# One PSUM chain for six of the seven products: the channel mixer's second matrix product, regrouped

## The chip, the cores and the metric

The kernel runs on one core of one Trainium2 chip. The metric is the device time in microseconds of one execution. Its engines work beside each other and meet by semaphores: PE (matrix products; PEld is its loading of weights), DVE and ACT (elementwise work, both can read PSUM), POOL (here mostly the issue of accumulating DMAs), and SP (the issue of plain DMAs). PSUM has 8 banks of 128 x 512 float32.

## The reference, cut to what matters

One layer on 512 tokens of 1024 channels: four token mixers, a gate, an output projection, then the channel mixer and the input embedding. The change is in the channel mixer's second product.

```python
hn = rms_norm(h, norm2_g[i])
ff = jnp.square(jax.nn.relu(jnp.einsum('bsd,df->bsf', hn, w_ff1[i])))
h = h + jnp.einsum('bsf,fd->bsd', ff, w_ff2[i])          # 512 x 4096 times 4096 x 1024

hg = rms_norm(h, norm3_g[i])
ple_gate = jax.nn.sigmoid(jnp.einsum('bsd,de->bse', hg, w_ple_gate[i]) + b_ple_gate[i])
h = h + ple_gate * jnp.einsum('bsq,qd->bsd', p[i], w_ple[i])
```

## The kernel before, in words

Float32 products are made of three: each operand is split into a high half that PE can multiply at full rate and a low half (the rest), and hi x hi, hi x lo and lo x hi are summed in PSUM. A weight is loaded as a tile of 128 x 1024; `split_piece` has ACT copy the high half (`wh<-raw` or `wh<-grow`, line 231) and DVE subtract it from the tile for the low half (`wl`, line 218).

The 4096 rows of `w_ff2` are worked in four groups g of 1024. In a group, the activations are a 2 x 2 grid of blocks (a11, a12, a21, a22: token half, row half), the weights too (11, 12, 21, 22: row half, column half), and the four blocks of the result take seven products of blocks, Q1 to Q7, instead of eight. A product multiplies one block or one sum of activations (`USES`; s1 to s4 are sums, made on DVE by `make`, then split into a tile `combo`) by one weight or one sum of weights (`SUMS`). A product is one step of 24 matmuls of 512 columns, on two weight tiles (h = 0, 1) and into two banks (i = 0, 1, a token block each).

The weights' sums are made by the DMAs: `load_piece` has SP load the first block plainly, and POOL add each further block with an accumulating DMA onto the same tile. `ONTO` lets a sum grow out of the tile of an earlier product once that is split: Q1 to Q5 to Q6 to Q4. Such tiles live in a ring of three (`grow`); all others in a ring of four (`raw`, `RAW = 4`), so that a plain load goes out when the low half of the fourth `raw` tile before it is made. SP and POOL each issue in the program's order.

`CHAIN` says which products share banks: a later product of a chain accumulates onto what the earlier one left. Before, Q1 and Q2 are chain 1; Q6, Q7 and Q4 chain 2; Q5 and Q3 chain 3. After each product `evac` adds the two banks onto the result tiles `ht[tb, half]` (tb: token block, half: columns) on DVE. Q1 alone is needed in six places, so its sum is kept over groups 0 to 2 (`first_q`), spread by six adds at the end of group 2 (`spread_q1`), and in group 3 spread from PSUM by six adds at once.

The order of the steps is written out: in groups 0 to 2 by `ORDER`, where the F steps are pieces of the first product of the next group; in group 3, the last, by `ORDER_LAST`, where U0 and U1 are the halves of the embedding's product `p W_p` (24 matmuls into four banks each, copied out by ACT). `MAKE` and `MAKE_LAST` say in which step an operand is made. In the middle of each step (`middle`) the low half of that operand follows, and up to two weights ahead are split.

Of the kernel before, what the change touches and what calls it, by code (L numbers as in the profile page):

```python
# [6 lines left out]
F32 = mybir.dt.float32  # L7
# [42 lines left out]
        "Q3": ("22",), "Q4": ("11", "12", "22", "21")}  # L50
ONTO = {"Q5": "Q1", "Q6": "Q5", "Q4": "Q6"}
ORDER = "Q1 F0 Q2 F1 Q5 F2 F3 Q6 F4 F5 Q7 F6 Q3 F7 Q4".split()
ORDER_LAST = "Q1 Q5 Q2 U0 Q6 Q3 Q7 U1 Q4".split()

MAKE = {"Q1": "s1", "Q2": "s2", "Q5": "s3", "F3": "s4", "Q6": "n22", "F5": "next a11", "Q4": "next a12"}
MAKE_LAST = {"Q1": "a12", "Q5": "s2", "Q2": "s4", "U0": "s3", "Q6": "n22"}
USES = {"Q1": "a11", "Q2": "a12", "Q5": "s1", "Q6": "s2", "Q7": "s3", "Q3": "s4", "Q4": "n22"}

# [20 lines left out]
def layout():  # L81


    out = []
    loads = []
    at = {}

    def flush():
        for i in range(len(at.setdefault("done", [])), len(out)):
            at["done"].append(i)  # L90
            loads.append(((i,), out[i][-1], None))

    tok = lambda n: [("tok", "w_in", COL[n], 512, (2 * i, 2 * i + 1), 1024) for i in range(4)]
    ch = lambda n, m: ("ch", "w_in", COL[n] + 128 * m, 1024)
    out += tok("a_v")
    out += [("gka", i, 816 if i < 2 else 544) for i in range(3)]
    out += tok("g_v")
    for m in range(4):
        out += [ch("a_q", m), ch("a_k", m)]
    for m in range(4):  # L100
        out += [ch("c_g", m), ch("c_a", m)]
    out += [ch("g_q", m) for m in range(2)]
    out += [ch("g_r", m) for m in range(4)]

    def branch(n):
        for m in range(8):
            out.append(("gate", n, m, 1024))
            if m % 2 == 0:
                out.append(("br", n, m // 2, 1024))

    branch(2)
    out += tok("sg_v")
    out += [ch("sg_u", m) for m in range(2)]
    flush()
    last = {}
    blocks = {}
    for p, e in gate_steps():
        if p == "S":
            out.append(ch("sg_u", e))
            flush()  # L120
        elif p[0] == "B":
            if int(p[1]) % 2 == 0:
                out.append(("br", e[0], 2 * e[1] + int(p[1]) // 2, 1024))
                flush()
        else:
            if p == "Q5":
                for b in ("11", "12", "21", "22"):
                    blocks[b] = len(out)
                    out.append(("gblock", *e, int(b[0]) - 1, int(b[1]) - 1, 1024))
                    at["done"].append(blocks[b])  # L130
            old = GATE_ONTO.get(p)
            new = GATE_SUMS[p][len(GATE_SUMS[old]) if old else 0:]
            loads.append((tuple(blocks[b] for b in new), 1024, last[old] if old else None))
            last[p] = len(loads) - 1
    out += [("ch", "w_out", 128 * m, 1024) for m in range(8)]
    flush()
    ff1 = lambda g, m: ("ch", "w_ff1", 1024 * g + 128 * m, 1024)
    out += [ff1(0, m) for m in range(8)]
    flush()
    for g in range(4):  # L140
        blocks = {}
        for e in ("11", "12", "21", "22"):
            for h in range(2):
                blocks[e, h] = len(out)
                out.append(("ff2", g, int(e[0]) - 1, int(e[1]) - 1, h, 1024))
                at["done"].append(blocks[e, h])
        last = {}
        for e in ORDER if g < 3 else ORDER_LAST:
            if e[0] == "F":
                out.append(ff1(g + 1, int(e[1])))  # L150
                flush()
            elif e[0] == "U":
                out.append(("tok", "w_ple", 512 * int(e[1]), 512, (0, 1), 1024))
                flush()
            else:
                for h in range(2):
                    old = ONTO.get(e) if g < 3 or e != "Q5" else None
                    new = SUMS[e][len(SUMS[old]) if old else 0:]
                    loads.append((tuple(blocks[n, h] for n in new), 1024, last[old, h] if old else None))
                    last[e, h] = len(loads) - 1  # L160
    for half in range(2):
        out += [("tok", "w_ple_gate", 512 * half, 512, (2 * i, 2 * i + 1), 1024) for i in (2, 3, 0, 1)]
    flush()
    return out, loads
# [9 lines left out]
def build(tc, x, w, vec, wa2, sgw, rows, rb, pt, out):  # L174
# [55 lines left out]
    def copy(o, a, **k):  # L230
        return ACT.activation(o, a, AF.Copy, **k)  # L231
# [1025 lines left out]
    def block(g, i, k):  # L1257

        return act[g, k][:, :, 256 * i:256 * i + 256]

    def make(g, n):

        sign = None
        if n == "a11":
            src = block(g, 0, 0)
        elif n == "a12":
            src = block(g, 0, 1)
        elif n == "n22":
            src, sign = block(g, 1, 1), -1.0
        else:  # L1270
            if n in ("s1", "s3"):
                combos[n] = lpool.tile([128, 4, 256], F32, tag=n, bufs=1, name=name(n))
            src = combos["s3" if n == "s3" else "s1"]
            if n == "s1":
                tt(src, block(g, 1, 0), block(g, 1, 1), OP.subtract)
            elif n == "s2":
                tt(src, block(g, 0, 0), src, OP.subtract)
            elif n == "s3":
                tt(src, block(g, 1, 0), block(g, 0, 0), OP.subtract)
            else:  # L1280
                tt(src, block(g, 0, 1), src, OP.subtract)
        t = lpool.tile([128, 2, 4, 256], F32R, tag="combo", bufs=4, name=name("combo"))
        if sign is None:
            copy(t[:, 0], src)
        else:
            copy(t[:, 0], src, scale=sign)
        yield "mid"
        if sign is None:
            tt(t[:, 1], src, t[:, 0].bitcast(F32), OP.subtract)
        else:  # L1290
            stt(t[:, 1], src, sign, t[:, 0].bitcast(F32), OP.mult, OP.subtract)
        combos[g, n] = t

    chains = {}
    CHAIN = {"Q1": 1, "Q2": 1, "Q5": 3, "Q3": 3, "Q6": 2, "Q7": 2, "Q4": 2}
    first_q = {}

    def add_to(tb, half, b, op=OP.add):
        tt(ht[tb, half], ht[tb, half], b, op)

    def spread_q1(i, t):
        add_to(i, 1, t, OP.subtract)
        add_to(2 + i, 1, t, OP.subtract)
        add_to(2 + i, 0, t)

    def product(g, n):
        j = base[n, g]
        c = CHAIN[n]
        fresh = n in ("Q1", "Q5", "Q6")

        def mms(_):
            if fresh:
                for i in range(2):
                    chains[c, i] = bank()
            t = combos.pop((g, USES[n]))
            for h in range(2):
                if h:
                    middle()
                hi, lo = parts[j + h]
                for i in range(2):  # L1320
                    b = chains[c, i]
                    for k in range(2):
                        s = [t[:, q, 2 * h + k, 128 * i:128 * i + 128] for q in range(2)]
                        cs = slice(512 * k, 512 * k + 512)
                        last = h == 1 and k == 1
                        mm(b, s[0], hi[:, cs], fresh and h == 0 and k == 0, False, skip_group_check=True)
                        mm(b, s[0], lo[:, cs], False, False, skip_group_check=True)
                        mm(b, s[1], hi[:, cs], False, last, skip_group_check=True)

        def evac(_):  # L1330
            for i in range(2):
                b = chains[c, i]
                if n == "Q1":
                    if g == 0:
                        first_q[i] = H()
                        copy(first_q[i], b)
                    elif g < 3:
                        tt(first_q[i], first_q[i], b, OP.add)
                    else:
                        spread_q1(i, b)  # L1340
                elif n == "Q2":
                    add_to(i, 0, b)
                elif n == "Q5":
                    add_to(2 + i, 1, b)
                elif n == "Q6" or n == "Q3":
                    add_to(i, 1, b)
                elif n == "Q7":
                    add_to(2 + i, 1, b)
                else:
                    add_to(2 + i, 0, b, OP.subtract)  # L1350

        step(j + 1, mms, evac, own=False)

# [58 lines left out]
    for g in range(4):  # L1412
        for e in ORDER if g < 3 else ORDER_LAST:
# [10 lines left out]
            else:  # L1424
                product(g, e)
            if g == 2 and e == "Q1":
                for i in range(2):
                    spread_q1(i, first_q.pop(i))
                start(load_last())
            if g == 2 and e == "F7":  # L1430
                hg = None
# [188 lines left out]
```

## Time and profile before

| what | value |
|---|---|
| runs: median of 3 (lowest to highest) | 986.85 us (986.17 to 987.85) |
| profiled execution | 986.83 us |
| its span in the trace | 985.1 us |
| PE busy | 965.7 us, 98% |
| DVE, ACT, POOL busy | 685.1, 457.6, 98.7 us |
| mean granted clock of PE | 0.994 of full |

The profiled execution is one run; its span is what the trace covers. A busy PE is not a PE at its peak, since records of matmuls overlap; the pace is read from where matmuls start. The group that the change touches most, the last one, begins near 876 us and ends with Q4 near 929 us.

### The profile page before, as it was taken

The page shows a single profiled execution, that of the slowest core. Times are in us where ns is not written, and L with a number is a line of the kernel's source. Part 1 is how long each engine was busy: PE and PEld are TensorE (multiplying, and loading weights), DVE is VectorE, ACT ScalarE, POOL GpSimd, SP SyncE. Part 2 cuts the span into 40 slices and gives each one's busy share as a digit, 9 for nine tenths or more (in the row PEclk, how much of TensorE's full clock was granted, in tenths as well). Part 3 has the DMA queues.
Part 4 walks back from the last instruction along what each step waited for, and adds up shares of the span by engine and source line. Part 5 has one row for each costly group of instructions (what it writes and reads, how often), then busy time and mean ns, then how long its engine had stood idle before and what let it go on. Part 6 is the DMA issues. An engine that isn't in the chain of part 4 may idle for free.

```text
span 985.1 us, 12890 instructions
## 1 busy us (share of the span) xinstructions
PE 965.7 (98%) x4990; PEld 820.5 (83%) x4990; DVE 685.1 (70%) x993; ACT 457.6 (46%) x685; POOL 98.7 (10%) x119
## 2 busy tenths in 40 slices
PE   8999999999999999999999999999999999999995
PEld 6977888887888898998999888888888888887885
DVE  7744897477899877877676653566576577578656
ACT  6563774235363435454554434435343345335633
POOL 5001000002121201110110000010001002011000
PEclk9999999999999999999999999999999999999998
DMA  6334322248598538756884233466468268677302
GB/s 242 121 117 128 118 82 81 86 111 188 110 237 229 141 107 199 182 168 157 220 250 129 89 129 104 92 145 170 129 171 193 99 179 183 199 176 185 133 22 86
DMA packets 43225, 144.96 MB, mean 147 GB/s; under 512 B 4859, under 2 KB 5276, under 8 KB 43164
## 3 DMA queue, kind: packets, MB, share of 16 engines
q1 hardware_dynamic: 32156, 104.29, 31.4%
q0 software_dynamic: 11008, 39.85, 22.3%
q8 instruction: 39, 0.64, 0.3%
q14 instruction: 22, 0.18, 0.1%
HBM read 139.92 MB, written 2.10 MB: 144 GB/s over the span
## 4 chain that ended last, share of the span: by engine, by line
PE 87%; DVE 6%; ACT 3%; issue 2%; DMA 1%; POOL 0%; SPq 0%; POOLq 0%; ACTq 0%; DVEq 0%
PE b L236 85%; DVE wl L218 2%; PE b L240 2%; DVE u L218 1%; ACT wh L231 1%; DVE ht L218 1%; DMA stack<-stack 1%; DVE u L222 0%; DMA raw<-w 0%; DVE gb L218 0%; DVE s L218 0%; ACT combo L231 0%; ACT ga L938 0%; DVE ht L222 0%; ACT u L231 0%
## 5 line engine op out<-in xcount | busy, mean ns | idle before, releaser
L236 PE MATMUL b<-x,wh 128*128 128x512 f32 (+1 forms) x1440 | 315.6, 363 | 2.5 <-DVE gb L218 2.5
L236 PEld LDWEIGHTS b<-x,wh 128*128 128x128 f32 x1440 | 243.9, 189 | 44.2 <-issue 4.5
L218 DVE TENSOR_TENSOR wl<-raw,wh 128x1024 fp32r<-128x1024 f32 (+2 forms) x150 | 182.3, 1223 | 74.3 <-ACT wh L231 73.0
L231 ACT ACTIVATE wh<-raw 128x1024 fp32r<-128x1024 f32 (+2 forms) x166 | 169.5, 1040 | 26.8 <-DMA raw<-w 18.4
L236 PE MATMUL b<-x,wl 128*128 128x512 f32 (+1 forms) x720 | 168.2, 361 | 0.0
L236 PE MATMUL b<-wh,combo 128*128 128x512 f32 x448 | 141.7, 390 | 0.5 <-DVE ht L218 0.5
L236 PEld LDWEIGHTS b<-x,wl 128*128 128x128 f32 x720 | 123.9, 189 | 20.8
L236 PEld LDWEIGHTS b<-wh,combo 128*128 128x128 f32 x448 | 84.1, 188 | 18.3 <-issue 0.9
L1240 ACT ACTIVATE act<-act 128x512 f32<-128x512 f32 x32 | 20.2, 632 | 147.7 <-DVE act L222 147.7
L236 PE MATMUL b<-wl,combo 128*128 128x512 f32 x224 | 87.5, 391 | 0.9 <-DVE wl L218 0.9
L236 PE MATMUL b<-u,wh 128*128 128x512 f32 x320 | 83.6, 391 | 0.0
L222 DVE SCALAR_TENSOR_TENSOR u<-pad,vecs,u 128x512 f32<-128x512 f32 x120 | 83.0, 745 | 0.0
L294 POOL DMA_DIRECT2D grow<-w x42 | 38.0, 953 | 361.6 <-DVE wl L218 307.3
L218 DVE TENSOR_TENSOR wl<-grow,wh 128x1024 fp32r<-128x1024 f32 x48 | 57.9, 1221 | 22.1 <-ACT wh L231 22.1
L236 PEld LDWEIGHTS b<-u,wh 128*128 128x128 f32 x320 | 59.3, 188 | 12.2 <-issue 0.3
L236 PE MATMUL b<-wh,x 128*128 128x512 f32 (+1 forms) x208 | 61.1, 374 | 0.0
L222 DVE SCALAR_TENSOR_TENSOR act<-b,v 128x512 f32<-128x512 f32 x32 | 22.0, 690 | 53.6 <-PE b L236 53.4
L236 PE MATMUL b<-wh,u 128*128 128x512 f32 (+1 forms) x192 | 54.1, 365 | 1.3 <-ACT wh L231 1.3
L231 ACT ACTIVATE wh<-grow 128x1024 fp32r<-128x1024 f32 x48 | 48.8, 1047 | 9.1 <-PE b L236 6.1
L236 PEld LDWEIGHTS b<-wl,combo 128*128 128x128 f32 x224 | 42.1, 188 | 10.7 <-DVE wl L218 2.1
L236 PE MATMUL b<-u,wl 128*128 128x512 f32 x160 | 46.7, 389 | 0.0
L236 PEld LDWEIGHTS b<-wh,x 128*128 128x128 f32 x208 | 38.1, 188 | 6.8
(196 smaller groups left out, 1177.4 us busy)
## 6 DMA issues: line engine op xcount, KB each, us to landing
raw<-w SPq DMA_DIRECT2D x161, 512.0 KB, 4.4
grow<-w POOLq DMA_DIRECT2D x42, 512.0 KB, 7.9
wl<-w POOLq DMA_DIRECT2D x16, 512.0 KB, 8.0
grow<-w SPq DMA_DIRECT2D x14, 512.0 KB, 5.6
raw<-w POOLq DMA_DIRECT2D x14, 512.0 KB, 7.5
h<-x SPq DMA_DIRECT2D x16, 256.0 KB, 6.9
v<-rb SPq DMA_DIRECT2D x8, 256.0 KB, 4.0
stack<-stack POOLq DMA_DIRECT2D x8, 256.0 KB, 3.7
```

The source lines that it names most:

```text
L218: return DVE.tensor_tensor(o, a, b, op=op)
L222: return DVE.scalar_tensor_tensor(o, a, s, b, op0=op0, op1=op1)
L231: return ACT.activation(o, a, AF.Copy, **k)
L236: PE.matmul(o, l, r, start=start, stop=stop, **k)
L240: PE.transpose(o, i, ident)
L294: POOL.dma_start(t[:, 0:n], w[i, :, 0:n], accum_op=OP.add)
L1240: ACT.activation(a, a, AF.Square)
```

## The change

Q1 now opens chain 2, in front of Q6, Q7 and Q4, and Q2 stands alone in chain 1. What Q1 is needed for is then in the chain's banks when Q6, Q7 and Q4 are evacuated, and every product is evacuated by two adds; `spread_q1` and `first_q` go. Q6 and Q7 are subtracted and Q4 is added; s2, s3 and s4 change sign or form to suit, and a22 is used in place of its negative. The last group's order is Q1 Q2 U0 Q5 Q6 Q3 Q7 U1 Q4 instead of Q1 Q5 Q2 U0 Q6 Q3 Q7 U1 Q4, its sums are made in other steps, and in it only Q4's weight sums still grow, out of Q6's: Q5's and Q6's are loaded on their own.

```diff
-ORDER_LAST = "Q1 Q5 Q2 U0 Q6 Q3 Q7 U1 Q4".split()
+ORDER_LAST = "Q1 Q2 U0 Q5 Q6 Q3 Q7 U1 Q4".split()
...
-MAKE_LAST = {"Q1": "a12", "Q5": "s2", "Q2": "s4", "U0": "s3", "Q6": "n22"}
-USES = {"Q1": "a11", "Q2": "a12", "Q5": "s1", "Q6": "s2", "Q7": "s3", "Q3": "s4", "Q4": "n22"}
+MAKE_LAST = {"Q1": "a12", "Q2": "s2", "U0": "s4", "Q5": "s3", "Q6": "a22"}
+USES = {"Q1": "a11", "Q2": "a12", "Q5": "s1", "Q6": "s2", "Q7": "s3", "Q3": "s4", "Q4": "a22"}
...
-                    old = ONTO.get(e) if g < 3 or e != "Q5" else None
+                    old = ONTO.get(e) if g < 3 or e == "Q4" else None
...
-                tt(src, block(g, 0, 0), src, OP.subtract)
+                tt(src, src, block(g, 0, 0), OP.subtract)
             elif n == "s3":
-                tt(src, block(g, 1, 0), block(g, 0, 0), OP.subtract)
+                tt(src, block(g, 0, 0), block(g, 1, 0), OP.subtract)
             else:
-                tt(src, block(g, 0, 1), src, OP.subtract)
+                tt(src, src, block(g, 0, 1), OP.add)
...
-        if sign is None:
-            tt(t[:, 1], src, t[:, 0].bitcast(F32), OP.subtract)
-        else:
-            stt(t[:, 1], src, sign, t[:, 0].bitcast(F32), OP.mult, OP.subtract)
+        tt(t[:, 1], src, t[:, 0].bitcast(F32), OP.subtract)
...
-    CHAIN = {"Q1": 1, "Q2": 1, "Q5": 3, "Q3": 3, "Q6": 2, "Q7": 2, "Q4": 2}
-    first_q = {}
+    CHAIN = {"Q2": 1, "Q1": 2, "Q6": 2, "Q7": 2, "Q4": 2, "Q5": 3, "Q3": 3}
...
-    def spread_q1(i, t):
-        add_to(i, 1, t, OP.subtract)
-        add_to(2 + i, 1, t, OP.subtract)
-        add_to(2 + i, 0, t)
...
-        fresh = n in ("Q1", "Q5", "Q6")
+        fresh = n in ("Q1", "Q2", "Q5")
...
-                if n == "Q1":
-                    if g == 0:
-                        first_q[i] = H()
-                        copy(first_q[i], b)
-                    elif g < 3:
-                        tt(first_q[i], first_q[i], b, OP.add)
-                    else:
-                        spread_q1(i, b)
-                elif n == "Q2":
+                if n in ("Q1", "Q2"):
                     add_to(i, 0, b)
                 elif n == "Q5":
                     add_to(2 + i, 1, b)
-                elif n == "Q6" or n == "Q3":
+                elif n == "Q6":
+                    add_to(i, 1, b, OP.subtract)
+                elif n == "Q3":
                     add_to(i, 1, b)
                 elif n == "Q7":
-                    add_to(2 + i, 1, b)
+                    add_to(2 + i, 1, b, OP.subtract)
                 else:
-                    add_to(2 + i, 0, b, OP.subtract)
+                    add_to(2 + i, 0, b)
...
             if g == 2 and e == "Q1":
-                for i in range(2):
-                    spread_q1(i, first_q.pop(i))
                 start(load_last())
```

POOL's accumulating DMAs of the last group. Before: first Q5's two weights, then the same two tiles grown for Q6, Q7's two, and the tiles grown again for Q4. The numbers tell tiles apart; what stands behind "waits" are semaphores, DMAHW of a plain load, DMASW of an accumulate, DVE of a low half.

```order
L294 DMA grow1286_7451<-w 128x1024 [waits DMAHW5_49]
L294 DMA grow1289_7458<-w 128x1024 [waits DMAHW6_49,DMASW6_49,DVE_49]
L294 DMA grow1286_7451<-w 128x1024 [waits DMASW0_49,DVE_49]
L294 DMA grow1289_7458<-w 128x1024 [waits DMASW1_49,DVE_49]
L294 DMA raw1321_7660<-w 128x1024 [waits DMAHW0_49,DMAHW2_49,DMASW5_49,DMAHW4_49,DMASW4_49,DVE_49]
L294 DMA raw1324_7667<-w 128x1024 [waits DMAHW5_49,DMAHW3_49,DMAHW7_49,DMAHW1_49,DVE_49]
L294 DMA grow1286_7451<-w 128x1024 [waits DMASW2_49,DVE_49]
L294 DMA grow1289_7458<-w 128x1024 [waits DMASW7_49,DMASW3_49,DVE_49]
```

The same stretch on POOL in the changed kernel: Q5's two (raw1296, raw1299), Q6's four (grow1305, grow1308), Q7's two, and Q4's two.

```order
L294 DMA raw1296_7519<-w 128x1024 [waits DMAHW4_49,DMAHW0_49,DVE_49]
L294 DMA raw1299_7526<-w 128x1024 [waits DMAHW1_49,DMAHW5_49,DMASW4_49,DVE_49]
L294 DMA grow1305_7564<-w 128x1024 [waits DMAHW2_49]
L294 DMA grow1305_7564<-w 128x1024 [waits DMASW2_49]
L294 DMA grow1308_7572<-w 128x1024 [waits DMAHW3_49,DMASW6_49]
L294 DMA grow1308_7572<-w 128x1024 [waits DMASW5_49,DMASW4_49]
L294 DMA raw1326_7661<-w 128x1024 [waits DMAHW6_49,DMASW0_49,DVE_49]
L294 DMA raw1333_7701<-w 128x1024 [waits DMASW7_49,DMAHW7_49,DMASW1_49,DVE_49]
L294 DMA grow1305_7564<-w 128x1024 [waits DMASW3_49,DVE_49]
L294 DMA grow1308_7572<-w 128x1024 [waits DMASW5_49,DVE_49]
```

Eight became ten; Q6's second accumulate on a tile stands directly behind the first on that tile and waits for a DMASW semaphore, not for DVE. On SP the plain loads stand in the order of the pieces: Q2's, U0's, Q5's two into `raw`, Q6's two into `grow`, Q3's two into `raw`; before it was Q5's two into `grow`, Q2's, U0's, Q3's.

DVE's work from Q1's step of the last group to the next product's evacuation. Before: the low half of operand a12, the low halves of two weights, the six adds of Q1's evacuation, then s2 and its low half, two weights, and the two adds of Q5's evacuation.

```order
L218 TENSOR_TENSOR combo1302_7551<-act1270_7327,combo1302_7551 128x1024
L218 TENSOR_TENSOR wl1306_7569<-grow1289_7458,wh1305_7568 128x1024
L218 TENSOR_TENSOR wl1308_7574<-raw1293_7492,wh1307_7573 128x1024
L218 TENSOR_TENSOR ht1018_5744<-ht1018_5744,b1303_7553 128x512
L218 TENSOR_TENSOR ht1029_5823<-ht1029_5823,b1303_7553 128x512
L218 TENSOR_TENSOR ht1004_5660<-ht1004_5660,b1303_7553 128x512
L218 TENSOR_TENSOR ht1024_5784<-ht1024_5784,b1304_7554 128x512
L218 TENSOR_TENSOR ht1043_5879<-ht1043_5879,b1304_7554 128x512
L218 TENSOR_TENSOR ht1012_5704<-ht1012_5704,b1304_7554 128x512
L218 TENSOR_TENSOR s11294_7508<-act1220_7044,s11294_7508 128x1024
L218 TENSOR_TENSOR combo1309_7597<-s11294_7508,combo1309_7597 128x1024
```

The same place on DVE in the changed kernel, to the two adds of Q2's evacuation.

```order
L218 TENSOR_TENSOR combo1300_7543<-act1268_7319,combo1300_7543 128x1024
L218 TENSOR_TENSOR wl1304_7561<-raw1287_7449,wh1303_7560 128x1024
L218 TENSOR_TENSOR wl1307_7569<-raw1291_7482,wh1306_7568 128x1024
L218 TENSOR_TENSOR ht991_5575<-ht991_5575,b1301_7545 128x512
L218 TENSOR_TENSOR ht998_5620<-ht998_5620,b1302_7546 128x512
L218 TENSOR_TENSOR s11292_7498<-s11292_7498,act1218_7036 128x1024
L218 TENSOR_TENSOR combo1309_7591<-s11292_7498,combo1309_7591 128x1024
L218 TENSOR_TENSOR wl1313_7609<-raw1296_7519,wh1312_7608 128x1024
L218 TENSOR_TENSOR wl1316_7615<-raw1299_7526,wh1315_7614 128x1024
L218 TENSOR_TENSOR ht991_5575<-ht991_5575,b1310_7593 128x512
L218 TENSOR_TENSOR ht998_5620<-ht998_5620,b1311_7594 128x512
```

Four adds are gone in front of s2, and the low halves of Q5's two accumulated weights (raw1296, raw1299) now stand in front of Q2's two adds.

## Rows read from the trace of the kernel before

**Rows 1.** The page's first part: busy time, share of the span, instructions.

```profile
PE 965.7 (98%) x4990; PEld 820.5 (83%) x4990; DVE 685.1 (70%) x993; ACT 457.6 (46%) x685; POOL 98.7 (10%) x119
```

**Rows 2.** A window: us; busy us of PE, PEld, DVE, ACT, POOL; clock, DMA, GB/s.

```profile
760.00:820.00 60.00, 60.00 (x267) 49.67 (x266) 39.62 (x45) 22.68 (x26) 3.54 (x4) 1.00 0.50 143
```

**Rows 3.** Waits of PE, 640 to 940 us: us in total, times, longest.

```profile
PE b L236 <- DVE wl L218: 0.9, 1, 0.9
PE b L236 <- DVE ht L218: 0.5, 1, 0.5
```

**Rows 4.** Timeline, 875 to 917 us: start, us, engine, what [idle before <- releaser].

```profile
875.61 1.22 DVE L218 TENSOR_TENSOR wl<-raw,wh 128x1024 fp32r<-128x1024 f32 x1
...
877.09 0.61 PE L236 MATMUL b<-wh,combo 128*128 128x512 f32 x2
...
877.77 0.61 PE L236 MATMUL b<-wh,combo 128*128 128x512 f32 x2
...
882.48 3.67 DVE L218 TENSOR_TENSOR ht<-ht,b 128x512 f32<-128x512 f32 x6
...
890.82 0.19 PEld L236 LDWEIGHTS b<-wl,combo 128*128 128x128 f32 x1 [1.25 <-DVE wl L218]
...
893.45 0.39 PE L236 MATMUL b<-wh,h 128*128 128x512 f32 x1
...
898.77 1.28 DVE L218 TENSOR_TENSOR ht<-ht,b 128x512 f32<-128x512 f32 x2
...
899.60 0.47 PE L236 MATMUL b<-wh,combo 128*128 128x512 f32 x1 [0.55 <-DVE ht L218]
...
916.67 0.39 PE L236 MATMUL b<-wh,h 128*128 128x512 f32 x1
```

**Rows 5.** Groups of instructions, 640 to 985 us: busy us, mean ns | idle before.

```profile
L218 DVE TENSOR_TENSOR wl<-raw,wh 128x1024 fp32r<-128x1024 f32 x56 | 67.2, 1219 | 15.7 <-ACT wh L231 15.6
L231 ACT ACTIVATE wh<-raw 128x1024 fp32r<-128x1024 f32 x56 | 56.6, 1048 | 5.0 <-PE b L236 3.7 <-DMA raw<-w 1.2
...
L218 DVE TENSOR_TENSOR ht<-ht,b 128x512 f32<-128x512 f32 x54 | 34.9, 680 | 0.9
...
L218 DVE TENSOR_TENSOR s<-act,s 128x1024 f32<-128x1024 f32 x8 | 9.7, 1215 | 0.0
```

**Rows 6.** The page's third part: DMA queue, packets, MB, share of 16 engines.

```profile
q1 hardware_dynamic: 32156, 104.29, 31.4%
q0 software_dynamic: 11008, 39.85, 22.3%
```

**Rows 7.** Plain loads (line 289) issued in the window 781.8 to 783.7 us.

```profile
L289 SPq DMA_DIRECT2D raw<-w x4: 382/403/729, 782.2 to 783.6; - x4
...
L289 SPq DMA_DIRECT2D grow<-w x1: 327/327/327, 781.8 to 781.8; - x1
...
DMA to landing us min/median/max: 3.6/5.2/7.8
```

**Rows 8.** SP's timeline from 870 us: the plain loads issued next.

```profile
876.85 15.41 SPq L289 DMA_DIRECT2D raw<-w  x4
```

**Rows 9.** The accumulate (line 294) issued at 857.6 us, alone.

```profile
DMA to landing us min/median/max: 5.4/5.4/5.4
```

**Rows 10.** The four accumulates (line 294) issued in the window 893 to 900 us.

```profile
DMA to landing us min/median/max: 5.7/7.3/9.6
```

**Rows 11.** POOL's timeline: the first and the last of those four.

```profile
894.87 0.88 POOL L294 DMA_DIRECT2D raw<-w  x1 [12.28 <-DVE s L218]
...
899.15 0.88 POOL L294 DMA_DIRECT2D grow<-w  x1 [0.26 <-DVE wl L218]
```

**Rows 12.** Windows near the start and at the end; columns as in rows 2.

```profile
8.00:11.20 3.20, 3.20 (x9) 2.46 (x9) 1.90 (x2) 2.72 (x5) 1.32 (x1) 0.50 1.04 408
11.20:20.00 8.80, 8.80 (x40) 7.28 (x39) 8.80 (x7) 8.80 (x14) 8.38 (x5) 1.00 0.71 260
...
977.00:980.00 3.00, 0.00 (x0) 0.00 (x0) 1.81 (x6) 0.93 (x3) 0.00 (x0) 0.52 0.23 87
```

More of the change, by code (lines that the diff above doesn't have):

```diff
@@ L52 @@
 ORDER = "Q1 F0 Q2 F1 Q5 F2 F3 Q6 F4 F5 Q7 F6 Q3 F7 Q4".split()
-ORDER_LAST = "Q1 Q5 Q2 U0 Q6 Q3 Q7 U1 Q4".split()
-MAKE = {"Q1": "s1", "Q2": "s2", "Q5": "s3", "F3": "s4", "Q6": "n22", "F5": "next a11", "Q4": "next a12"}
-MAKE_LAST = {"Q1": "a12", "Q5": "s2", "Q2": "s4", "U0": "s3", "Q6": "n22"}
-USES = {"Q1": "a11", "Q2": "a12", "Q5": "s1", "Q6": "s2", "Q7": "s3", "Q3": "s4", "Q4": "n22"}
+ORDER_LAST = "Q1 Q2 U0 Q5 Q6 Q3 Q7 U1 Q4".split()
+MAKE = {"Q1": "s1", "Q2": "s2", "Q5": "s3", "F3": "s4", "Q6": "a22", "F5": "next a11", "Q4": "next a12"}
+MAKE_LAST = {"Q1": "a12", "Q2": "s2", "U0": "s4", "Q5": "s3", "Q6": "a22"}
+USES = {"Q1": "a11", "Q2": "a12", "Q5": "s1", "Q6": "s2", "Q7": "s3", "Q3": "s4", "Q4": "a22"}
 GATES = ((1, 0), (1, 1), (0, 0), (0, 1), (3, 0), (3, 1))
@@ L1261, in make @@
     def make(g, n):
[L1263 to L1269, printed above, removed]
+        if n[0] == "a":
+            src = block(g, int(n[1]) - 1, int(n[2]) - 1)
         else:
@@ L1276, in make @@
             elif n == "s2":
-                tt(src, block(g, 0, 0), src, OP.subtract)
+                tt(src, src, block(g, 0, 0), OP.subtract)
             elif n == "s3":
-                tt(src, block(g, 1, 0), block(g, 0, 0), OP.subtract)
+                tt(src, block(g, 0, 0), block(g, 1, 0), OP.subtract)
             else:
-                tt(src, block(g, 0, 1), src, OP.subtract)
+                tt(src, src, block(g, 0, 1), OP.add)
         t = lpool.tile([128, 2, 4, 256], F32R, tag="combo", bufs=4, name=name("combo"))
-        if sign is None:
-            copy(t[:, 0], src)
-        else:
-            copy(t[:, 0], src, scale=sign)
+        copy(t[:, 0], src)
         yield "mid"
-        if sign is None:
-            tt(t[:, 1], src, t[:, 0].bitcast(F32), OP.subtract)
-        else:
-            stt(t[:, 1], src, sign, t[:, 0].bitcast(F32), OP.mult, OP.subtract)
+        tt(t[:, 1], src, t[:, 0].bitcast(F32), OP.subtract)
         combos[g, n] = t
     chains = {}
-    CHAIN = {"Q1": 1, "Q2": 1, "Q5": 3, "Q3": 3, "Q6": 2, "Q7": 2, "Q4": 2}
-    first_q = {}
+    CHAIN = {"Q2": 1, "Q1": 2, "Q6": 2, "Q7": 2, "Q4": 2, "Q5": 3, "Q3": 3}
     def add_to(tb, half, b, op=OP.add):
         tt(ht[tb, half], ht[tb, half], b, op)
-    def spread_q1(i, t):
-        add_to(i, 1, t, OP.subtract)
-        add_to(2 + i, 1, t, OP.subtract)
-        add_to(2 + i, 0, t)
     def product(g, n):
@@ L1332, in evac @@
                 b = chains[c, i]
-                if n == "Q1":
-                    if g == 0:
-                        first_q[i] = H()
-                        copy(first_q[i], b)
-                    elif g < 3:
-                        tt(first_q[i], first_q[i], b, OP.add)
-                    else:
-                        spread_q1(i, b)
-                elif n == "Q2":
+                if n in ("Q1", "Q2"):
                     add_to(i, 0, b)
```

## The prediction, made before the changed kernel ran

> **What bounds the kernel now.** I read the page first: PE is busy 98% of the span [rows 1]. So a gain has to come out of PE's waiting, and anything that makes PE wait costs in full. Next the windows, by stage: over the first three groups of the channel mixer's second product PE is busy for all of every window (60.00 of 60.00 us in the one shown), at granted clock 1.00 [rows 2]. Then who waited for whom, from 640 us to 940 us: PE has two waits only, 0.9 us for a low half (wl) of a weight and 0.5 us for an add into ht [rows 3]. Last the timeline of that place, the last group [rows 4]: Q1's evacuation is six adds on DVE, 3.67 us; DVE is then late for all that is queued behind it, and Q2's matmuls stop until 890.82 (weight loads idle 1.25 us). After U0, Q6 waits until 899.60 for a bank that Q2's evacuation, begun at 898.77, frees.
>
> The pace: three matmuls take 0.68 us (877.09 to 877.77) [rows 4], so a step of 24, which every product and every U has, takes 5.44. U0's first matmul is at 893.45 and U1's at 916.67 [rows 4]: 23.22 us for four steps that need 21.76, 1.46 lost. With the 1.25 before U0, all that the last group can give back is 2.7 us.
>
> **The change part by part.** *Groups 0 to 2.* Q1's separate sum (two ACT copies, four adds) and its spreading (six adds) become six adds in all: 4 adds less, 0.68 us each [rows 5]. PE waits for none of them there [rows 2, 3], so I cost this at nothing. The negated a22 loses its scalar operand and the sums their sign; counts stay, and PE's matmuls keep their number. With no wait of PE there, less work on DVE can gain nothing. The long chain now holds two of the eight banks from Q1 to Q4; should a fresh product wait for a bank there as Q6 did once, it would cost 0.5 a group [rows 3], 1.5 at most. I take 0, since F steps lie between the products of these groups.
>
> *Last group, DVE.* Q1's evacuation is two adds instead of six: 2.7 us less in front of s2. Walked forward from 882.48 with the trace's durations (add 0.68, sum and low half 1.22, ACT's high half 1.05 [rows 5]), Q2's weights are split in time, and so PE's two stalls go. If nothing else were late, the gain would be those 2.7 us less about 0.5: Q6's second weight, split after s3, would have its low half at 901.0, and Q6 wants it at 900.6. (Q1 starts three steps and 1.25 us before 893.45, at 875.9; Q6 is fifth now, so it starts at 897.6, is half done at 900.4, and its second matmul on the new weight is at 900.6.)
>
> *Last group, weights.* This is the part that decides. Before, Q6's two sums grew out of Q5's tiles: one accumulating DMA each, and those tiles were loaded early into their own ring. Now Q5's are built in the four raw slots, and Q6's from nothing: one plain load and two accumulating ones each, the second on the same tile. The order on POOL shows what that means: the second accumulate of grow1305 waits for the first one's semaphore, the two for grow1308 stand behind it in the queue, and Q7's behind those. Four accumulates become six, in three links that cannot overlap.
>
> When it starts: Q5's first load needs the slot of Q1's second weight, whose low half DVE makes at 875.61, 1.22 long. SP issued the load for that slot at 876.85 before [rows 4, 8], and does so now. Q5's second load needs the next slot, about 878.0, and Q6's two stand behind it on SP's queue, with no wait that is still open, about 0.4 apiece later. Q3's two follow between 881.5 and 882.6, when DVE is through with the two low halves ahead of the adds at 882.48.
>
> What a transfer costs: five plain loads issued from 781.8 to 783.6 landed 3.6 us after the first issue and 7.8 after the last, at 785.4 and 791.4, so 1.5 us each behind the first [rows 7]. An accumulate alone landed 5.4 after its issue [rows 9]. Four issued from 894.87 to 899.15 landed 5.7 after the first and 9.6 after the last [rows 10, 11], at 900.6 and 908.7: 2.7 us each behind the first. The page's totals say the same: 104.29 MB at 31.4% is 1.55 us per 512 KB, 39.85 MB at 22.3% is 2.9 us [rows 6].
>
> So: Q5's first load lands at 876.85 + 3.4 to 3.6 = 880.3. Behind it lie five plain loads (7.5 us) and three accumulates, Q5's two and Q6's first (8.1 us). Q6's first accumulate is the last of them to be issued, so it lands at about 896. Its tile's second one is issued then and lands at 901.4. The other tile's first, issued 1 us behind it, lands 2.7 later, 904.1, and only then its second one is issued: 909.5. ACT's high half takes 1.05 and DVE's low half 1.22 [rows 5]: 911.8, against 900.6, so Q6 stops for about 11.2 us in all (the first of its two weights and the late banks of Q5 wait inside that time). Bounds: 891 instead of 896 if the accumulates overtook every plain load after the first two (880.3 + 2.7 to the first one's data, + 8.1); 896.7 by the page's 1.55 and 2.9. Each later link is at least 5.4, at most some 8.
>
> What is late next: DVE and ACT stand still meanwhile and have caught up when Q6 goes on; Q3, Q7 and U1 then run at pace, their loads being queued already. So no second loss.
>
> *The clock.* After the last matmul, with PE idle, the granted clock falls to 0.52 (977 to 980). Near the start it was 0.50 from 8.0 to 11.2, and PE did 9 matmuls in 3.2 us, then 40 in 8.8 us at 1.00 (2.4 GHz): 9 are worth 2.0 us, so that stretch cost 1.2 [rows 12]. A stop of over 5 us in Q6 has no like in the last group of before, whose stalls of about 1 us left the clock at 1.00. I take one such stretch, 1.2; the ends are 0 and 1.7 (half of such a stretch). The Trainium skill, TensorE: Matmul & The Clock Gate, "HAM oscillation", says that a matmul loop that waits on a DMA is throttled and starts its next work cold; by it the 1.2 is due, without it the sum is 1.2 less.
>
> **The sum.** Gone: 2.7. New: 11.2 + 1.2. Net +9.7 us on the profiled execution's 986.83, whose span is 985.1; it agrees with the runs' median of 986.85. Forecast 996.5.
>
> **The rivals.**
> *The chain of loads is hidden (faster).* If Q6's second weight has landed by 899.5, ACT and DVE set the time, and 2.7 less 0.5 is gained: 984.6. For it: before, PE waited for no transfer there [rows 3], though Q5's sums took a load and an accumulate too. Against it: even with each accumulate at its lone 5.4 and no other traffic, Q6's first is issued at 883, the links end at 888.4, 894.8 and 900.2, and the low half is ready at 902.5. The point is 899.5.
> *The chain costs only what DVE gives back.* That lone sum: 1.9 lost, 2.7 gained, 986.0, within the noise. Against it: ten transfers lie in those 20 us.
> *Accumulates first.* With 891 instead of 896 the stop is 6.2, with the clock 7.4, less 2.7: +4.7, 991.5. For it: in the row of four accumulates plain loads were few, and the trace doesn't show who goes first. The Trainium skill, DMA: Bandwidth & Descriptors, "Queues, rings and completion order", has the engines take turns between queues; by it neither side overtakes and 896 stands. The row of 2.7 each, with hardly a plain load beside it, doesn't decide that.
> *Accumulates slowed at each link.* Q7's two loads and the instruction fetches come in between; with links of 7.5 instead of 5.4 the last lands at 913.7, the stop is 15.4, and the sum +13.9: 1000.7. Against it: with POOL held at each link, few transfers are in flight at once.
> *Bank instead of weight.* Q5 takes the banks of Q2, whose adds now stand behind Q5's own late second weight on DVE; Q5 stops for some 3 us. It is inside Q6's stop unless that is short; alone it would give 987.
>
> **How the numbers follow.** Forecast (a stop of 9 to 13 us) 0.48; accumulates first, or otherwise a stop of 5 to 9, 0.25; slowed links 0.11; bank alone 0.04; hidden 0.06; evened out by what DVE gives back 0.06. A measurement of this kernel can tell 0.2%, 2 us, from no change. Faster by more: 0.06. Within: 0.06 and half of the bank's, 0.08. Slower: 0.86. The range leaves out the hidden case, the evened one, and the worst of the slowed links: 987.5 to 1001.
>
> **What would show it.** After: ACT's wh<-grow waits for a DMA in the last group, PE idle some 10 us in one or two pieces around Q6, waiting for wl<-grow; POOL's issues on grow 5 us or more apart in three steps; two adds after Q1 and no wait in Q2. Wrong if Q6's second accumulate is issued before 890, if PE's stop is under 4 us, or if PE waits anywhere in groups 0 to 2.

## The result and the profile after

The changed kernel takes 1001.26 us (median of 4 runs, 1001.18 to 1003.32) where the kernel before, run beside it, takes 986.51. The ratio is 1.0154, with a 95% interval of 1.0139 to 1.0169: slower, as forecast, but by some 15 us where 9.7 were forecast. 1001.26 lies 0.3 us above the top of the range. The profiled execution is the 1001.26 one; its span is 999.5, against 985.1 before, 14.4 more. (The new chain holds four of the seven products, Q1, Q6, Q7 and Q4; the title's six is the number of places in which Q1 is needed.)

First the page of after, parts 1 and 3, against [rows 1, 6]: as many matmuls as before, eight DVE instructions fewer, two accumulating DMAs more on POOL and, by the bytes, two plain loads more (each 512 KB).

```profile
PE 971.7 (97%) x4990; PEld 824.5 (82%) x4990; DVE 680.5 (68%) x985; ACT 457.2 (46%) x683; POOL 100.6 (10%) x121
...
q1 hardware_dynamic: 32444, 105.34, 31.0%
q0 software_dynamic: 11296, 40.90, 22.3%
```

The waits of PE in after, 640 to 985 us (us in total, times, longest), against [rows 3]. All of them lie in the last group; groups 0 to 2 have none, as before.

```profile
PE b L236 <- DVE ht L218: 4.6, 1, 4.6
PE b L236 <- ACT wh L231: 4.2, 1, 4.2
PE b L236 <- DVE wl L218: 1.2, 2, 0.8
```

The timeline of PE in after, the last group (start, us, engine, line, what [idle before <- releaser]), which answers to [rows 4]. The first row is U0's first matmul, the last U1's.

```profile
886.63 0.39 PE L236 MATMUL b<-wh,h 128*128 128x512 f32 x1
...
896.83 0.77 PE L236 MATMUL b<-wh,combo 128*128 128x512 f32 x1 [4.60 <-DVE ht L218]
...
906.37 0.50 PE L236 MATMUL b<-wl,combo 128*128 128x512 f32 x1 [0.76 <-DVE wl L218]
...
913.38 0.80 PE L236 MATMUL b<-wh,combo 128*128 128x512 f32 x1 [4.18 <-ACT wh L231]
...
914.64 0.80 PE L236 MATMUL b<-wl,combo 128*128 128x512 f32 x1 [0.46 <-DVE wl L218]
...
915.24 1.05 PE L236 MATMUL b<-wh,combo 128*128 128x512 f32 x2
...
930.61 0.39 PE L236 MATMUL b<-wh,h 128*128 128x512 f32 x1
```

From U0 to U1 there are now five steps (U0, Q5, Q6, Q3, Q7), 27.2 us at the pace of 5.44; they take 930.61 - 886.63 = 43.98. So 16.8 us are lost here, where 1.46 were lost before. The stop comes in four pieces: Q5 for banks, then Q6 for its first new weight, its second one's high half and its low half. Behind it the matmuls themselves are slow, as the windows of after show (columns as in rows 2): the granted clock is 0.51 of full speed, the lower of the two levels, and 13 matmuls fill 5 us where the pace gives 22. The clock fell once before, behind Q5's wait (0.60 and 0.72); what that cost lies inside Q6's wait for its weights.

```profile
895.00:900.00 5.00, 3.17 (x8) 2.52 (x9) 3.88 (x5) 1.55 (x3) 1.77 (x2) 0.60 0.80 243
900.00:905.00 5.00, 5.00 (x18) 3.96 (x16) 0.77 (x1) 1.49 (x3) 0.00 (x0) 0.72 1.01 184
...
910.00:915.00 5.00, 1.15 (x2) 0.65 (x3) 1.64 (x2) 2.73 (x3) 0.43 (x2) 0.81 1.06 206
915.00:920.00 5.00, 5.00 (x13) 3.87 (x13) 5.00 (x6) 3.18 (x4) 0.76 (x1) 0.51 1.06 211
```

What PE waited for is told by the chain of work that ended last, after (start, us, what), and by POOL's timeline.

```profile
886.02 11.23 issue
897.26 1.77 POOL grow L294 x2
899.03 7.69 issue
906.73 5.46 DMA grow<-w
...
913.36 1.24 DVE wl L218
914.64 21.57 PE b L236 x83
```

```profile
884.24 0.87 POOL L294 DMA_DIRECT2D raw<-w  x1 [2.86 <-DVE ht L218]
884.93 1.09 POOL L294 DMA_DIRECT2D grow<-w  x1
897.26 1.77 POOL L294 DMA_DIRECT2D grow<-w  x2 [11.24 <-DMA grow<-w]
906.73 0.87 POOL L294 DMA_DIRECT2D grow<-w  x1 [7.70 <-DMA grow<-w]
```

Q6's accumulates are issued at 884.93 (its first tile's first), 897.26 and 897.89 (that tile's second, the other's first) and 906.73 (the other's second). POOL stands for 11.24 and for 7.70 us, both times for a landing on grow. The landings, one row for the accumulates issued in each of the windows 884 to 885.2, 897 to 898 and 906.5 to 906.8:

```profile
DMA to landing us min/median/max: 9.4/10.7/12.0
...
DMA to landing us min/median/max: 6.7/7.6/8.6
...
DMA to landing us min/median/max: 5.5/5.5/5.5
```

So the three links end at 896.97, at 903.9 and 906.45, and at 912.19. ACT, whose timeline has its two waits for these tiles, begins the last high half at 912.27, DVE the low half at 913.36, and PE goes on at 914.64.

```profile
903.99 1.06 ACT L231 ACTIVATE wh<-grow 128x1024 fp32r<-128x1024 f32 x1 [3.51 <-DMA grow<-w]
...
912.27 1.06 ACT L231 ACTIVATE wh<-grow 128x1024 fp32r<-128x1024 f32 x1 [3.68 <-DMA grow<-w]
```

### The profile page after: what moved, and what is told of

Its sections match the earlier page's. It is cut to its first block, busy times and chain, and to the rows that moved or that the text cites. A ratio compares the mean times of both kernels' runs of the same rounds, so it can differ in the third digit from the quotient of the medians.

```text
span 999.5 us, 12886 instructions
## 1 busy us (share of the span) xinstructions
PE 971.7 (97%) x4990; PEld 824.5 (82%) x4990; DVE 680.5 (68%) x985; ACT 457.2 (46%) x683; POOL 100.6 (10%) x121
## 4 chain that ended last, share of the span: by engine, by line
PE 86%; DVE 5%; issue 4%; ACT 2%; DMA 2%; POOL 0%; SPq 0%; POOLq 0%; ACTq 0%; DVEq 0%
PE b L236 84%; PE b L240 2%; DVE wl L218 2%; DVE u L218 1%; ACT wh L231 1%; DMA stack<-stack 1%; DMA grow<-w 1%; DVE u L222 0%; DMA raw<-w 0%; DVE gb L218 0%; POOL grow L294 0%; ACT ga L938 0%; DVE ht L218 0%; DVE ht L222 0%; ACT u L231 0%
## 5 line engine op out<-in xcount | busy, mean ns | idle before, releaser
L218 DVE TENSOR_TENSOR wl<-raw,wh 128x1024 fp32r<-128x1024 f32 (+2 forms) x152 | 184.7, 1223 | 82.2 <-ACT wh L231 80.8
L231 ACT ACTIVATE wh<-raw 128x1024 fp32r<-128x1024 f32 (+2 forms) x168 | 171.6, 1039 | 39.0 <-DMA raw<-w 30.5
L236 PE MATMUL b<-wh,combo 128*128 128x512 f32 x448 | 146.1, 400 | 8.8 <-DVE ht L218 4.6
L236 PEld LDWEIGHTS b<-wh,combo 128*128 128x128 f32 x448 | 86.7, 194 | 28.1 <-issue 5.0
L236 PE MATMUL b<-wl,combo 128*128 128x512 f32 x224 | 89.5, 400 | 1.2 <-DVE wl L218 1.2
L218 DVE TENSOR_TENSOR wl<-grow,wh 128x1024 fp32r<-128x1024 f32 x46 | 55.5, 1220 | 30.1 <-ACT wh L231 30.1
L236 PEld LDWEIGHTS b<-u,wh 128*128 128x128 f32 x320 | 59.3, 188 | 12.2 <-issue 0.3
L231 ACT ACTIVATE wh<-grow 128x1024 fp32r<-128x1024 f32 x46 | 46.8, 1047 | 16.1 <-DMA grow<-w 11.8
```

The lines of the kernel that those rows point to most:

```text
L218: return DVE.tensor_tensor(o, a, b, op=op)
L236: PE.matmul(o, l, r, start=start, stop=stop, **k)
```

## The experiments

Theory A: the time goes to Q6's weights, whose accumulates follow one another, each behind the landing of the last, and to the clock that falls in the stop; the regrouping itself is a gain. Rivals: the new long chain or the new order costs by itself (banks, DVE), or the accumulates are slow because of what else is transferred, not because they are in series. As a yardstick I use the time from U0's first to U1's first matmul, 27.2 us at pace and 43.98 in after. U0's own start differs by up to 3 us between the profiled executions (883.46 in e5, 886.63 in after), which this leaves out. It differs because group 0 itself begins earlier or later: from its first matmul (627.17 in e5, 630.34 in after) to U0 both take 256.29 us.

**e1: after, with Q6's weights grown out of Q5's tiles again.**

```
-                    old = ONTO.get(e) if g < 3 or e == "Q4" else None
+                    old = ONTO.get(e) if g < 3 or e != "Q5" else None
```

> The changed kernel with one line undone: in the last group Q6's weight sums grow out of Q5's tiles again, as before. Theory A (the serial accumulates of Q6's weights cost the time): the stop in Q6 goes and DVE's relief is left, 984 to 985.5 us, PE without waits over 1 us in the last group. Theory B (the regrouping itself costs: banks held longer, Q5 waiting for Q2's banks, the order of the steps): it stays near the changed kernel, above 995 us.

Measured: 983.17 us, ratio 0.9973 (0.996 to 0.9985). The whole loss is gone and a small gain stands in its place. The timeline of PE in e1 has one wait, 0.55 us, and U0 to U1 takes 28.05:

```profile
886.03 0.39 PE L236 MATMUL b<-wh,h 128*128 128x512 f32 x1
...
900.57 0.50 PE L236 MATMUL b<-wl,combo 128*128 128x512 f32 x1 [0.55 <-DVE wl L218]
...
914.08 0.39 PE L236 MATMUL b<-wh,h 128*128 128x512 f32 x1
```

So the one line of the rule for the loads carries the loss. It also puts Q5's tiles back into the ring `grow`, so this run alone does not tell Q6's late weights from Q5's; e6 does. The wait that is left is the 0.5 us of Q6's low half behind s3 that the prediction's walk along DVE had found.

**e2: e1 with the order of the last group before (Q1, Q5, Q2, U0, ...).**

```
-ORDER_LAST = "Q1 Q2 U0 Q5 Q6 Q3 Q7 U1 Q4".split()
+ORDER_LAST = "Q1 Q5 Q2 U0 Q6 Q3 Q7 U1 Q4".split()
-MAKE_LAST = {"Q1": "a12", "Q2": "s2", "U0": "s4", "Q5": "s3", "Q6": "a22"}
+MAKE_LAST = {"Q1": "a12", "Q5": "s2", "Q2": "s4", "U0": "s3", "Q6": "a22"}
```

> The regrouping alone: Q1 opens the long chain and Q1's evacuation has two adds, but the last group keeps the order of before (Q1 Q5 Q2 U0 Q6 ...) and its weights grow as before. Theory A: the two stalls of before go with the four adds, about 2 us faster than before, 984 to 985.5 us; the order is worth under 0.5 us against the run with the new order and grown weights. Theory B (the new order is what relieves DVE): this is no faster than before, 986 to 987 us.

Measured: 986.41 us, ratio 0.9992 (0.998 to 1.0005): no gain. A's figure was missed and B's, 986 to 987, held, though not for B's reason. From Q1 to U1 of the last group e2 takes 40.35 us, before 40.71. The timeline of PE in e2 shows a wait inside U0:

```profile
898.35 0.50 PE L236 MATMUL b<-wh,h 128*128 128x512 f32 x1 [1.96 <-DVE ht L218]
```

I had not counted banks here. In the code Q1's two stay with the long chain until Q4 and Q5's two until Q3; with Q2's two, only two of the eight are left for U0's four, and the third waits for Q2's adds: twelve matmuls of U0, six to a bank, stand in front of the wait. Of these two orders the regrouping needs the new one, in which U0 precedes Q5. A gain of DVE time alone was turned into a wait for a bank.

**e3: the kernel before, with only the changed rule for the loads.**

```
-                    old = ONTO.get(e) if g < 3 or e != "Q5" else None
+                    old = ONTO.get(e) if g < 3 or e == "Q4" else None
```

> The kernel before with the weights of the change alone: Q5's and Q6's sums of the last group are loaded on their own, order and chains as before. Theory A, worked out from the transfers: Q5 stands second here, so its loads go out a step pair earlier and Q6's accumulates have the queue for themselves; the last lands near 900 us of the span and is wanted by DVE at about 901: 986 to 990 us. Theory C (three links in a row cost their 14 to 15 us wherever Q5's loads lie): 996 to 1002 us.

Measured: 998.89 us, ratio 1.0135 (1.0117 to 1.0153). A missed and C's figure held: the loads alone cost 12.2 us, most of the 14.8. The timeline of POOL in e3 shows the same three links:

```profile
884.14 0.87 POOL L294 DMA_DIRECT2D grow<-w  x1 [22.96 <-DMA grow<-w]
891.20 1.78 POOL L294 DMA_DIRECT2D grow<-w  x2 [6.18 <-DMA grow<-w]
...
901.63 0.87 POOL L294 DMA_DIRECT2D grow<-w  x1 [8.66 <-DMA grow<-w]
```

I had expected little because I took 5.4 us a link; they took 6.8, then 7.7 and 9.5 for the two tiles, and 5.5, and the last landed at 907.1 instead of near 900. And the stop stood in another place: PE waited 12.26 us once, for adds into ht.

```profile
910.29 0.76 PE L236 MATMUL b<-wh,combo 128*128 128x512 f32 x1 [12.26 <-DVE ht L218]
```

In before's order Q6's weights are split in Q2's step, so DVE stands at their low halves with Q2's adds queued behind it, and Q6 lacks its banks. DVE's timeline in e3:

```profile
908.32 1.22 DVE L218 TENSOR_TENSOR wl<-grow,wh 128x1024 fp32r<-128x1024 f32 x1 [7.02 <-ACT wh L231]
909.46 1.27 DVE L218 TENSOR_TENSOR ht<-ht,b 128x512 f32<-128x512 f32 x2
```

From 910.29 to U1 (928.60) three products, 16.32 at pace, take 18.31: 2.0 us went to the clock behind this stop (0.56 from 910 to 915). It is one chain of loads with two faces: with the name of an add as releaser it is still the load.

**e4: after, POOL's four accumulates for Q6 in another order: the first of each tile, then the second of each.**

```
+    second = []
...
-        for i in srcs:
+        for i in srcs[:1]:
             POOL.dma_start(t[:, 0:n], w[i, :, 0:n], accum_op=OP.add)
+        if onto is None and len(srcs) == 2:
+            second.append((t, srcs[1]))
+            if len(second) == 2:
+                for u, i in second:
+                    POOL.dma_start(u[:, 0:n], w[i, :, 0:n], accum_op=OP.add)
```

> The changed kernel with POOL's four accumulates for Q6 in another order: the first one of each tile, then the second one of each. Same transfers, same bytes. Theory A (the links' waits for landings set the time): the last lands at about 906 instead of 912 us of the span, 995 to 996.5 us. Theory D (the transfers' total work on the DMA engines sets it, however they are queued): no change, 1000.5 to 1002 us.

Measured: 994.49 us, ratio 1.0078 (1.0058 to 1.0098). With the same transfers and bytes, and two links instead of three, about 7 us came back, so the serial order counts by itself and D fell. How the rest divides between the links that are left and the traffic, this run doesn't show. The timeline of POOL in e4 (line 295 the firsts, 300 the seconds):

```profile
884.42 0.87 POOL L295 DMA_DIRECT2D grow<-w  x1 [1.21 <-DMA grow<-w]
885.92 0.87 POOL L295 DMA_DIRECT2D grow<-w  x1 [0.64 <-DMA grow<-w]
896.01 0.88 POOL L300 DMA_DIRECT2D grow<-w  x1 [9.21 <-DMA grow<-w]
899.67 0.87 POOL L300 DMA_DIRECT2D grow<-w  x1 [2.79 <-DMA raw<-w]
```

The last of them landed at 905.6 instead of 912.19: 6.6 us earlier, 5.4 of it measured from U0's first matmul (885.45 here). U0 to U1 took 38.32, 5.66 less than in after: the stop in Q6 ended 3.19 us earlier behind U0, and from its end (910.27) to U1 the work took 13.50 instead of 15.97. The time went half a us below A's figure. Of the 11.1 us still lost, a part is Q5's wait for banks (5.1 here), which e6 shows alone.

**e5: after, with 16 extra matmuls into a spare bank in the middle of Q6; what they compute is not used.**

```
+        if g == 3 and n == "Q6":
+            idle = bank()
+            for k in range(FILLERS):        # FILLERS = 16
+                mm(idle, t[:, 0, 0, 0:128], parts[j][0][:, 0:512], k == 0, k == FILLERS - 1)
```

> The changed kernel with 16 extra matmuls of Q6's first weight into a spare bank, whose result nobody reads, placed in the middle of Q6 where PE stood idle from 909.2 to 913.4 us of the span. At pace they take 3.6 us, inside that wait. Theory A (the rest of the loss behind the wait is the granted clock, 0.51 from 915 to 920 us, where 12 matmuls took 5.1 us instead of 2.7): PE goes on at full clock, 2 to 2.8 us are gained, 998.3 to 999.3 us. Theory E (PE is slow there since weights and operands still come late): no gain, 1000.8 to 1002 us, and still 0.43 us per matmul.

Measured: 998.38 us, ratio 1.0137 (1.0116 to 1.0158). That interval overlaps after's, so the time alone decides nothing; the trace does, for its execution: the five runs lie between 995.12 and 1001.01, and the profiled one is the 995.12, so how much the fillers give in every run is not shown. The windows of e5 (its U0 lies 3.17 us earlier than after's):

```profile
910.00:915.00 5.00, 4.23 (x19) 3.34 (x19) 5.00 (x6) 4.52 (x5) 0.88 (x1) 1.00 1.06 211
915.00:920.00 5.00, 5.00 (x24) 4.14 (x23) 3.99 (x5) 0.00 (x0) 0.00 (x0) 1.00 1.04 283
```

And its timeline of PE, the end of the stop and U1:

```profile
910.97 0.50 PE L237 MATMUL b<-wl,combo 128*128 128x512 f32 x1 [0.77 <-DVE wl L219]
...
924.48 0.39 PE L237 MATMUL b<-wh,h 128*128 128x512 f32 x1
```

The same work, from the end of the stop to U1, took 13.51 us instead of after's 15.97: 2.46 us were the clock's, within the 2 to 2.8 expected. The pace gives 13.37, 0.14 less than the 13.51. E fell: the weights were there.

**e6: after, with Q6's two weights loaded earlier, right behind Q1's.**

```
+        if j == EARLY[0]:
+            for q in EARLY[1:]:
+                load_tile(q)
+                early_done.add(q)
...
```

EARLY[0] is Q1's second weight of the last group, the others are Q6's two, which are left out at their old place.

> The changed kernel with the same ten accumulates and plain loads, but Q6's two tiles loaded right behind Q1's weights (where the kernel before loaded Q5's), so that the three links begin near 853 us of the span instead of 878. Theory A (when the links begin decides, since they are too long only for the lead they had): no stop in Q6, 983 to 985.5 us, with at most a short wait for Q5's second accumulated weight. Theory F (one more accumulate and two more loads per tile cost DMA time that other weights then lack): 988 to 996 us.

Measured: 989.56 us, ratio 1.0041 (1.0025 to 1.0056). Q6 no longer stops: its links took 5.4, then 9.3 and 9.0 for the two tiles, and 9.5, but began at 857.48 and ended at 885.89, in time. That is worth 11.7 us by the medians and 8.9 from U0 to U1 (the profiled execution is the slowest of the six, 991.94). But Q5 stops, A's 983 to 985.5 was missed, and F's figure, 988 to 996, held; F's reason isn't needed for it, since after has the same stop with Q6's tiles loaded late. The timelines of PE and DVE in e6, and its windows:

```profile
896.62 0.77 PE L238 MATMUL b<-wh,combo 128*128 128x512 f32 x1 [4.76 <-DVE ht L220]
```

```profile
894.66 1.23 DVE L220 TENSOR_TENSOR wl<-raw,wh 128x1024 fp32r<-128x1024 f32 x1 [2.39 <-ACT wh L233]
895.80 1.28 DVE L220 TENSOR_TENSOR ht<-ht,b 128x512 f32<-128x512 f32 x2
```

```profile
895.00:900.00 5.00, 3.38 (x8) 2.74 (x9) 3.88 (x5) 1.75 (x3) 0.87 (x1) 0.58 0.64 138
900.00:905.00 5.00, 5.00 (x18) 3.96 (x18) 3.12 (x4) 3.48 (x6) 1.75 (x2) 0.74 0.91 155
```

Q5's second accumulated weight is late; its low half stands on DVE in front of Q2's adds, and Q5 needs their banks. That is the stop of 4.60 that after has at 896.83 as well, where it is hidden: Q6 would have waited as long anyway. Here Q5's first matmul is due at 891.70 and comes 4.9 us later, and with the clock at 0.58 and 0.74 the work behind it takes 2.9 more (U0 to U1 35.04, 27.2 at pace).

**e7: e1, with s3 made in Q6's step instead of Q5's, behind Q6's low half.**

```
-MAKE_LAST = {"Q1": "a12", "Q2": "s2", "U0": "s4", "Q5": "s3", "Q6": "a22"}
+MAKE_LAST = {"Q1": "a12", "Q2": "s2", "U0": "s4", "Q6": "s3", "Q3": "a22"}
```

> The run with grown weights and the new order, with operand s3 made in Q6's step instead of Q5's, and a22 in Q3's instead of Q6's, so that Q6's second weight is split before s3. There PE waited 0.55 us in Q6 for that weight's low half, behind s3 on DVE. Theory A: that wait goes, 0.4 to 0.6 us less than the run with grown weights: 982.4 to 982.9 us on a chip where that one takes 983.2. Theory G: another operand comes late in its place (s3 for Q7): same or slower.

Measured: 982.58 us, ratio 0.9967 (0.9956 to 0.9978), as A expected, and no wait of PE from 640 to 960 us; U0 to U1 takes 27.33, against 28.05 in e1. This is the fastest version. Its interval overlaps e1's, so that it beats e1 is shown by the trace alone; that it beats both kernels of the case is shown by the time.

## Why the prediction was wrong in size

**What held.** The place and the mechanism. Six accumulates in three links, POOL waiting for landings at 897.26 and 906.73, ACT's wh<-grow waiting for a DMA, no wait in groups 0 to 2: each is in the trace of after, and e1, e4 and e6 show it by experiment. The DVE term, "all that the last group can give back is 2.7 us", came out at 2.63: 1.17 in front of U0 (in before Q1 begins at 875.96, three steps need 16.32, U0 begins at 893.45; the prediction's 1.25 is the idle time of the weight loads) and 1.46 behind it. The groups put at nothing were nothing: from group 0's first matmul to the last group's Q1 both kernels take 245.41. And e1, without the loads, has the gain: from Q1 to U1 it takes 38.93, before 40.71, 1.8 less against a forecast of 2.2.

**The step that failed** is the sum "11.2 + 1.2", both terms too small: the stop took each later link at the price of a lone accumulate, and the clock took one stretch of the start. The ends for the clock, "0 and 1.7", did not hold what came (half of that 3.2 us stretch is 1.6, besides). Against the span's 14.4, which 9.7 undershot by 4.7:

- *The stop*: Q6's second matmul on the new weight was due 13.83 us behind U0's first (U0 and Q5, 10.88, and 13 matmuls of Q6, 2.95), at 900.46; it came at 914.64, so 14.18 instead of 11.2, 3.0 more. The chain landed at 912.19 for the forecast 909.5: 0.97 because its first link ended at 896.97 and not 896; 1.25 because the second took 6.65 and not 5.4; 0.57 because POOL needed about 0.28 after each landing to issue; the other tile's first landed 2.54 behind, for 2.7. The price 5.4 was that of a lone accumulate [rows 9]; it held for the last link only (5.46), which had nothing ahead of it in flight and three more accumulates issued 0.55 to 1.65 us behind it. Beside the second lay Q7's plain loads (landed at 897.94 and 899.56) and the other tile's first accumulate, issued 0.63 behind it. I had the bound, "at most some 8", and took the low end of it for every link.
- *The clock*: 2.60 instead of 1.2, 1.4 more. From 914.64 to U1 the work is 2.49 of Q6 and two products, 13.37 at pace, and took 15.97. I had priced one stretch at the clock's lower level by the kernel's start [rows 12], where 9 matmuls were done in 3.2 us. Here the level lasted longer: 13 matmuls, worth 2.95, filled the 5.00 us from 915 on, which alone is 2.05. e5, with the clock held at 1.00, gave 2.46 of it back. The Trainium skill, TensorE: Matmul & The Clock Gate, "HAM oscillation", has a matmul loop that waits on a DMA start its next work cold; the trace agrees, at 0.51.
- *The rest*: 0.07 more by the DVE term, 0.21 less since group 0 began that much earlier (630.34 for 630.55), and 0.46 more behind U1 (68.89 us to the end of the span, 68.43 before; e1 has 68.42). The 0.46 lie behind the last instruction on DVE, which starts 63.95 us behind U1 in both; the five runs with the changed loads have 4.9 to 5.0 us there, the four without 4.4 to 4.5. Why stays open. 2.98 + 1.40 + 0.07 - 0.21 + 0.46 is 4.70.

**The rivals.** *Hidden* and *evened out* fell: the last landing was 912.19, the point 899.5. *Accumulates first* fell: Q6's first landed at 896.97, not 891. The Trainium skill, DMA: Bandwidth & Descriptors, "Queues, rings and completion order", has each DMA engine take turns between the queues it has work for. The trace goes with it: a plain load issued at 882.38 landed at 895.65, between accumulates that were issued behind it, at 884.24 and 884.93, and landed at 893.67 and 896.97. *Slowed links* came nearest, at 1000.7, in part by luck: the second link was slowed, but its 7.5 for each and its stop of 15.4 were too much, and the clock, which it had at 1.2, made up for it. *Bank instead of weight* was seen as it is: Q5 stopped for 4.60, inside Q6's stop; alone, in e6, it cost 4.9 instead of some 3, and 2.9 for the clock, so 987 was too little for a like reason: the stop was too short and priced without the clock that falls with it.

**Open.** That plain loads lengthen a link is argued from the traces, not tested by taking the loads away. Accumulates with little or nothing ahead of them landed in 5.1 to 5.7 us, and those behind it did not slow the last link; with others ahead or plain loads in flight they took 5.7 to 13.5.

## What to carry to other kernels

When a change turns one transfer onto a tile into several that depend on each other, count the links in the queue and give each link the price of its own surroundings, and look whether another tile's first link can be issued between (e4: 5.7 us from U0 to U1 for the order of two issues). Charge a stop on PE like these, 4.2 to 12.3 us, with what the clock costs behind it, here 2.0 to 2.9 us. Before a chain is made longer, count the banks that every open chain holds at the next product: in e2 that ate the gain.

## What was not expected of the hardware

- The clock fell after pieces of 4.2 us (after) and 4.8 us (e6) of waiting, and the loss behind them, 2.60 and 2.9 us, was larger than the start of the kernel shows. Behind e3's wait of 12.3 us it was 2.0, no larger for the longer wait.
- 16 matmuls whose output nobody reads, in the middle of the stop, kept the granted clock at 1.00 in the profiled execution and made the work after it 2.46 us shorter, at no price of their own that the trace shows: PE still waited 0.42 us for the weight behind them.
- Accumulating transfers of the same 512 KB landed 5.4 us after their issue, alone (before, 857.6), and up to 13.5 behind a queue of others (e4, 885.92).
